# Five expert pairs written to DRAM and gathered back, weight loads in another order, and three small moves, in a two-layer decoder kernel

## The chip, the cores and the metric

The kernel runs on one core of a Trainium2 chip. A core has TensorE (PE in the profile: matmuls; PEld is its weight load), VectorE (DVE), ScalarE (ACT), GpSimd (POOL) and SyncE (SP); 16 DMA engines move data between DRAM and the on-chip memory SBUF. PSUM holds matmul results. The metric is device time in microseconds (us), lower is better.

## The reference

Two decoder layers over 512 tokens of width 1024. Each layer has a mixer (stick-breaking attention and gated linear attention) and then a mixture of 32 SwiGLU experts with hidden width 256, of which each token uses the two best of one group. A vector `c` gives shift, scale and gate of both sub-layers (adaLN).

```python
def reference(x, c, w_ada, b_ada, norm_mix, norm_ffn, ...):
    c_act = jax.nn.silu(c)
    for l in range(DEPTH):
        mod = (c_act @ w_ada[l] + b_ada[l])[:, None, :]
        shift_m, scale_m, gate_m, shift_f, scale_f, gate_f = jnp.split(mod, N_MOD, axis=-1)
        h = rms_norm(x, norm_mix[l]) * (1.0 + scale_m) + shift_m
        x = x + gate_m * hybrid_mixer(h, w_in[l], ...)
        h = rms_norm(x, norm_ffn[l]) * (1.0 + scale_f) + shift_f
        x = x + gate_f * hierarchical_moe(h, w_router_grp[l], ..., w_gate[l], w_up[l], w_down[l])
    return x
# in hierarchical_moe, for each group g:
    a = jnp.einsum('nd,edf->nef', hf, w_gate[g])
    u = jnp.einsum('nd,edf->nef', hf, w_up[g])
    y = y + jnp.einsum('nef,efd->nd', jax.nn.silu(a) * u * comb[:, g, :, None], w_down[g])
```

## The kernel before

The expert stage `moe` runs once in each layer. Its tokens are sorted into slots: each expert has 64 slots, two experts make a pair of 128 slots, and there are 16 pairs, numbered from 0. `logits` transposes the tokens (tiles `xT`, copied out of PSUM by DVE) and multiplies them with the router's weights; DVE then picks group and experts and counts slots (`slot`). Meanwhile ACT writes the normed tokens (`xn`) and GpSimd's queue sends them to DRAM (`xg`). `fetch` gathers the 128 rows of a pair from `xg` by an indirect DMA of GpSimd; empty slots fetch nothing. `gather` transposes them (`g`, `gT`).

For pair i, PE then runs three kinds of work. `hidden` multiplies the pair's tokens with gate and up weights of both experts (I call this gu(i); its weights are tile `wgu`, 2 MiB for an expert, 5 buffers). `turn` transposes the hidden values. `down` multiplies them with the down weights (d(i); tile `wd`, 1 MiB for an expert, 4 buffers), and DVE scales the result by routing weight and gate (`o`). `combine` brings the rows back to their tokens: ACT and GpSimd split `o` into a high and a low part (`ohi`, `olo`), and PE multiplies both with a 0/1 matrix `oT` made by `places`, into 8 pieces `y` of 128 tokens by 512 columns, 16 matmuls (y(i)); DVE adds the pieces to `x`. The order on PE in the loop is d(i-1), gu(i), y(i-1), the latter mixed with transposes for later pairs.

All weights come by SP's queue, which issues in program order. The list `queue` fixes that order; an entry (0, e) is the gate and up weights of expert e, (1, e) its down weights. Nine entries are asked for before the stage begins (five of `wgu`, four of `wd`, 14 MiB); each later one waits for a buffer that gu or d has let go. The scheduler of the framework orders the instructions inside an engine, within what the code pins (`kept_dma`, `pm`).

At the start of layer 0, `mixer` loads x, the rows of small vectors (`load_rows`: biases and norm gains, transposed by PE into `cols`) and the adaLN weights (`wada`), squares x on ACT, and projects.

Of the kernel before, what the change touches and what calls it, by code (L numbers as in the profile page):

```python
# [9 lines left out]
F = mybir.dt.float32  # L10
R = mybir.dt.float32r
BF = mybir.dt.bfloat16
I32 = mybir.dt.int32
# [7 lines left out]
P = 128  # L21
# [2 lines left out]
SBW, GKW, GVW, RANK, NIN = 512, 256, 512, 16, 3088  # L24
NE, FE, CAP = 32, 256, 64
NX = 16


@with_exitstack
def hybrid_decoder_kernel(ctx, tc, x, c, w_ada, b_ada, norm_mix, norm_ffn, w_in, w_gk2, b_gk, q_gain,  # L30
# [36 lines left out]
    def att(name="att"):  # L67
        return bank(name, "att", 3)
# [17 lines left out]
    def kept_dma(eng, o, a):  # L86

        tc.keep_in_program_order(eng.dma_start(o, a))
# [98 lines left out]
    def load_rows():  # L187

        rows = rowt[0]([100, P], name="rows")
        for l in range(L):  # L190
            for i in range(2):
                r = 32 * l + 16 * i
                kept_dma(SY, rows[r:r + 16], b_ada[l, 3 * D * i:3 * D * i + 2 * D].rearrange("(r p) -> r p", p=P))
        kept_dma(SY, rows[64:80], norm_mix.rearrange("l (k p) -> (l k) p", p=P))
        kept_dma(SY, rows[80:96], norm_ffn.rearrange("l (k p) -> (l k) p", p=P))
        kept_dma(SY, rows[96:100], b_gk.rearrange("l (g p) -> (l g) p", p=P))
# [14 lines left out]

    xs = dram.tile([S, D], F, name="xs")
    xg = dram.tile([S, D], F, name="xg")

    mod = [const.tile([P, 6, KT], F, name=f"mod{l}") for l in range(L)]
    gates, gms, rowt = {}, {}, {}
# [66 lines left out]
    def mixer(l, xt, ss, x_src, pool, later):  # L283
# [42 lines left out]
        lrT = const.tile([RANK, S], F, name="lrT", tag="lrT")  # L326


        if l == 0:
            for tt in range(NT):  # L330
                for q in range(2):
                    square(ss, xt, tt, q)
        if l:

            ps = att("warm")
            for _ in range(16):
                pm(ps[:, 0:P], ident, ident, True, True)
        pin = tiny.tile([P, 1], F, name="pin")
        A.copy(pin, ss[:, 0, 0:1])
        tc.keep_in_program_order(A.preload_act_table_set("natural_log_exp_and_others"))  # L340
        rs = inv_rms(ss, G if l else A)
        xn = []
        for tt in range(NT):
            t = xt[tt // 2][:, tt % 2]
            xn.append(t if l == 0 else mixs([P, D], name="xn"))
            if l == 0:
                V.tensor_scalar(xn[tt], t, rs[:, tt:tt + 1], None, op0=OP.mult)
            else:
                V.tensor_scalar(xn[tt][:, 0:512], t[:, 0:512], rs[:, tt:tt + 1], None, op0=OP.mult)
                A.activation(xn[tt][:, 512:D], t[:, 512:D], AF.Copy, scale=rs[:, tt:tt + 1])  # L350
        if l:

            for i in range(2):
# [487 lines left out]
    def logits(l, xt, s2):  # L841


        wr, lc, _ = route[l]
        lgT = misc("lgT")
        for k in range(KT):
            ps = att("xT")
            for tt in range(NT):
                T.transpose(ps[:, P * tt:P * tt + P], xt[tt // 2][:, tt % 2, P * k:P * k + P], ident)
            t = s2([P, S], name="xT")  # L850
            V.tensor_copy(t, ps)
            o = 64 * (k % 2)
            mm(lgT[o:o + 64], wr[:, 36 * k:36 * k + 64], t, k < 2, k >= KT - 2)
        t = s2([P, S], name="lgT")
        V.tensor_copy(t, lgT)
        lg = route[l][2] = att("lg")[:, 0:NT * 36].rearrange("p (t e) -> p t e", t=NT)
        for tt in range(NT):
            mm(lg[:, tt], t[:, P * tt:P * tt + P], two_parts, tt == 0, True)

    def moe(l, xt, ss, pool):  # L860
        wgu = slots(pool, "wgu", 5, 16384)
        wd = slots(pool, "wd", 4, 8192)
        g4 = slots(pool, "gT", 3, 4096)
        rows_ = slots(pool, "rows", 4, 4096)
# [28 lines left out]
        wr, lc, lg = route.pop(l)  # L893
        rs = inv_rms(ss)

        for tt in range(NT):
            xn = rows_([P, KT, P], name="xn")
            normed = A.activation(xn, xt[tt // 2][:, tt % 2].rearrange("t (p k) -> t k p", k=KT), AF.Copy,
                                  scale=rs[:, tt:tt + 1])
# [137 lines left out]
        def down(hT, ws, i=None):  # L1037

            n = len(ws)
            r = slice(0, 64 * n)  # L1040
            parts, last = [], None
            if i == NE // 2 - 1:

                last = wgu([P, 2, 2, 512], R, name="last")
            for q in range(2):
                pd = bank("d", "dy", 4)
                for j in range(2):
                    for e in range(n):
                        pm(pd[64 * e:64 * e + 64], hT[:, j, 64 * e:64 * e + 64],
                           ws[e][:, D * j + 512 * q:D * j + 512 * q + 512], j == 0, j == 1)  # L1050
                o = ot([P, 512], name="o")
                gate = gates[l, 5][r, 512 * q:512 * q + 512]
                if i is None:
                    V.tensor_tensor(o[r], pd[r], gate, op=OP.mult)
                    parts.append(o)
                else:
                    V.scalar_tensor_tensor(o, pd, cws[:, i:i + 1], gate, op0=OP.mult, op1=OP.mult)  # L1057
                    if last is not None:
                        hi, lo = last[:, q, 0], last[:, q, 1]
                    else:  # L1060
                        hi, lo = ohl([P, 512], R, name="ohi"), ohl([P, 512], R, name="olo")
                    A.activation(hi, o, AF.Copy)  # L1062
                    (G if last is None else V).tensor_tensor(lo, o, hi.bitcast(F), op=OP.subtract)  # L1063
                    parts.append((hi, lo))
            return parts
# [29 lines left out]
        def combine_last(pairs):  # L1095
# [17 lines left out]
            yield  # L1113
            for n, u in ((0, 5), (0, 6), (1, 0), (1, 1), (0, 7), (1, 2), (1, 3), (1, 4), (1, 5), (1, 6), (1, 7)):
                unit(n, u)

        def spread(slot, slot0):

# [80 lines left out]
        with tc.issue_after(listed.ins), tc.issue_after(normed.ins):  # L1199
# [14 lines left out]
            V.tensor_tensor(e2, e2, den, op=OP.mult)  # L1214
            V.tensor_tensor(cw[:, :, 1:2], e2, gw, op=OP.mult)
            dump(f"cw{l}", cw)
            exw = tmp.rearrange("p t k e -> p (t k) e")
            V.tensor_tensor(exw, ex.rearrange("p t k e -> p (t k) e"), cw.rearrange("p t k -> p (t k)")[:, :, None].to_broadcast([P, NT * 2, NE]), op=OP.mult)
        cws = pool.tile([P, NE // 2], F, name="cws")
# [17 lines left out]
        for _ in rest:  # L1237
            pass
        gT1, second = gather(fetched[1:2])
        hs = None  # L1240
        for i in range(NE // 2):
            while not {(0, 2 * i), (0, 2 * i + 1)} <= set(loaded):
                load_weights(1)
            if i % 2 == 0:
                now = gT
                if i < NE // 2 - 2:
                    gT, rest = gather(fetched[i + 2:i + 4])
                    fetched += [fetch(idx[:, j:j + 1]) for j in range(i + 4, min(i + 6, NE // 2))]

            if i:  # L1250
                part = places(i - 1), down(hT, [loaded.pop((1, e)) for e in (2 * i - 2, 2 * i - 1)], i - 1)
            *_, hs = hidden(gT1 if i == 1 else now, 0 if i < 2 else P * (i % 2), [loaded.pop((0, e)) for e in (2 * i, 2 * i + 1)])
            load_weights(4)
            if i == 1:
                overflow_lists()
            if i == NE // 2 - 1:
                break

            if i == 0:
                for _ in second:  # L1260
                    pass
                weights_by_slot()
            for u in range(4):
                for v in range(2):
                    if i:
                        combine(2 * u + v, *part)
                next(rest, None)
                if u == 2:
                    hT = turn(hs)
        last = []  # L1270
        end = combine_last([part, last])
        next(end)
# [93 lines left out]
```

## Time and profile before

| | us |
|---|---|
| median of 3 runs | 1230.94 (1230.35 to 1233.77) |
| profiled execution, its own time | 1231.71 |
| its span, first to last instruction | 1229.6 |
| PE busy | 1176.4 (96%) |
| DVE busy | 687.8 (56%) |
| ACT busy | 472.6 (38%) |
| POOL busy | 188.2 (15%) |

The profile is one execution. Busy shares are averages over stages with different limits: the expert stages lie at about 350 to 630 us (layer 0) and 940 to 1230 us (layer 1), and in them the DMA engines are busy all the time as well.

### The profile page before, as it was taken

Reading aid. Unit: us, or ns where it says so; the run is one execution under the profiler, and the core shown is the slowest. Engines: PE = TensorE matmul, PEld = TensorE weight load, DVE = VectorE, ACT = ScalarE, POOL = GpSimd, SP = SyncE. Lnnn points to the kernel's source line nnn. Section 1 sums busy time; section 2 is a strip of 40 time slices with the busy share of each in tenths; the row PEclk is TensorE's granted clock in tenths of the full one; section 3 lists DMA queues with packets and bytes.
Section 4 is the critical chain, followed back from the end, with each engine's and each line's share of the span. In section 5 each row is a group of like instructions: output and inputs, shape, how many; then the busy total and the mean of one; then the engine's idle time right before and its main releaser. Section 6 shows DMA issues by size and latency. Waiting matters only on the chain. (4 is left out here: it accounts for less than half of the span.)

```text
span 1229.6 us, 17212 instructions
## 1 busy us (share of the span) xinstructions
PE 1176.4 (96%) x6441; PEld 743.4 (60%) x6441; DVE 687.8 (56%) x1343; ACT 472.6 (38%) x940; POOL 188.2 (15%) x222
## 2 busy tenths in 40 slices
PE   4999999999989999999999997999999999999996
PEld 2687766666765444444478785666776744444443
DVE  4475545465864555555566563445846565555553
ACT  4376646453242111111155764454624411111111
POOL 1000010011302222221110001001310222222110
PEclk8999999999999999999999999999999999999999
DMA  9653665643687999999445354564129599999981
GB/s 299 211 181 110 202 166 155 198 152 96 258 353 265 410 411 420 420 419 418 178 168 167 96 172 108 171 179 127 56 103 383 212 397 420 420 418 420 420 328 69
DMA packets 105902, 312.27 MB, mean 254 GB/s; under 512 B 12852, under 2 KB 49912, under 8 KB 81240
## 3 DMA queue, kind: packets, MB, share of 16 engines
q1 hardware_dynamic: 96920, 289.62, 63.3%
q0 software_dynamic: 8896, 21.52, 5.2%
q8 instruction: 52, 0.85, 0.3%
q14 instruction: 34, 0.28, 0.1%
HBM read 311.08 MB, written 8.40 MB: 260 GB/s over the span
## 5 line engine op out<-in xcount | busy, mean ns | idle before, releaser
L78 PE MATMUL gu<-wgu,gT 128*64 128x512 f32 x1024 | 225.4, 592 | 0.1
L74 PE MATMUL proj<-whl,hh 128*128 128x512 f32 (+2 forms) x768 | 220.6, 370 | 0.1
L78 PEld LDWEIGHTS gu<-wgu,gT 128*64 128x64 f32 x1024 | 75.4, 137 | 143.7 <-issue 142.2
L74 PEld LDWEIGHTS proj<-whl,hh 128*128 128x128 f32 x768 | 133.9, 190 | 35.0 <-issue 13.3
L1070 DVE TENSOR_TENSOR x<-y,x 128x512 f32<-128x512 f32 x240 | 148.2, 679 | 0.9 <-PE y L78 0.9
L74 PE MATMUL proj<-whl,hl 128*128 128x512 f32 (+2 forms) x384 | 138.6, 362 | 0.0
L1025 DVE TENSOR_TENSOR hs<-hs,gu 128x256 f32<-128x256 f32 x32 | 13.5, 421 | 201.2 <-ACT hs L1024 201.2
L78 PE MATMUL d<-wd,hT 128*64 128x512 f32 x512 | 116.9, 598 | 1.4 <-ACT hT L1034 1.4
L1063 POOL TENSOR_TENSOR olo<-o,ohi 128x512 fp32r<-128x512 f32 x60 | 77.0, 1285 | 263.4 <-ACT ohi L1062 263.4
L96 DVE TENSOR_TENSOR whl<-raw,whl 128x512 fp32r<-128x512 f32 (+2 forms) x128 | 73.2, 574 | 78.0 <-ACT whl L95 67.6
L78 PE MATMUL y<-ohi,oT 128*128 128x512 f32 x240 | 104.5, 436 | 0.0
L95 ACT ACTIVATE whl<-raw 128x512 fp32r<-128x512 f32 (+2 forms) x128 | 66.4, 524 | 76.6 <-PE proj L74 64.7
L78 PE MATMUL y<-olo,oT 128*128 128x512 f32 x240 | 94.2, 393 | 0.0
L74 PEld LDWEIGHTS proj<-whl,hl 128*128 128x128 f32 x384 | 72.4, 189 | 14.2 <-issue 4.3
L1024 ACT ACTIVATE hs<-gu 128x256 f32<-128x256 f32 x32 | 12.3, 385 | 168.4 <-PE gu L78 168.4
L78 PEld LDWEIGHTS d<-wd,hT 128*64 128x64 f32 x512 | 33.9, 136 | 62.2 <-issue 48.1
L78 PEld LDWEIGHTS y<-ohi,oT 128*128 128x128 f32 x240 | 45.4, 189 | 31.7 <-issue 26.0
L1003 ACT ACTIVATE gT<-g,mod 128x256 f32<-128x256 f32 (+1 forms) x72 | 39.0, 544 | 62.6 <-DVE gT L1005 62.3
L1062 ACT ACTIVATE ohi<-o 128x512 fp32r<-128x512 f32 x60 | 37.8, 630 | 61.7 <-DVE o L1057 61.7
L1057 DVE SCALAR_TENSOR_TENSOR o<-d,cws,gate_f 128x512 f32<-128x512 f32 x64 | 47.6, 746 | 21.4 <-PE d L78 21.4
L733 POOL TENSOR_TENSOR raw<-raw,gate_m 128x1024 f32<-128x1024 f32 x16 | 40.4, 2533 | 122.9 <-DMA raw<-in_w_out_dram 63.1
L78 PE MATMUL ada<-wada,ct 128*32 128x512 f32 x320 | 50.2, 600 | 5.3 <-DMA wada<-in_w_ada_dram 3.8
(332 smaller groups left out, 1935.0 us busy)
## 6 DMA issues: line engine op xcount, KB each, us to landing
wgu<-in_w_gate_dram SPq DMA_DIRECT2D x64, 1024.0 KB, 9.6
wgu<-in_w_up_dram SPq DMA_DIRECT2D x64, 1024.0 KB, 11.8
wd<-in_w_down_dram SPq DMA_DIRECT2D x64, 1024.0 KB, 11.0
wada<-in_w_ada_dram SPq DMA_DIRECT2D x96, 512.0 KB, 5.1
raw<-in_w_in_dram SPq DMA_DIRECT2D x80, 256.0 KB, 4.5
raw<-in_w_out_dram SPq DMA_DIRECT2D x16, 512.0 KB, 5.0
raw<-in_w_in_dram SPq DMA_DIRECT2D x32, 128.0 KB, 4.0
xg<-xn POOLq DMA_DIRECT2D x8, 512.0 KB, 5.9
```

The costliest lines, as they stand in the source:

```text
L74: T.matmul(o, a, b, start=start, stop=stop, skip_group_check=True)
L78: tc.keep_in_program_order(T.matmul(o, a, b, start=start, stop=stop, skip_group_check=True))
L95: A.activation(hi, src, AF.Copy)
L96: eng.tensor_tensor(lo, src, hi.bitcast(F), op=OP.subtract)
L733: G.tensor_tensor(t, t, gates[l, 2][:, None, cols].to_broadcast([P, 2, 512]), op=OP.mult)
L1003: A.activation(o, src, AF.Identity, scale=m, bias=b)
L1024: A.activation(hs[r], gu[r, 0:256], AF.Silu)
L1025: V.tensor_tensor(hs[r], hs[r], gu[r, 256:512], op=OP.mult)
L1057: V.scalar_tensor_tensor(o, pd, cws[:, i:i + 1], gate, op0=OP.mult, op1=OP.mult)
L1062: A.activation(hi, o, AF.Copy)
L1063: (G if last is None else V).tensor_tensor(lo, o, hi.bitcast(F), op=OP.subtract)
L1070: V.tensor_tensor(xc, ps, xc, op=OP.add)
```

## The change

There are four parts.

1. The first five pairs (`NY = 5`) are not combined by matmuls. Their scaled rows `o` are written to a DRAM tile `ys` by GpSimd's queue. Near the end of the stage, `take_back` gathers each token's row from `ys` by an indirect DMA (8 gathers in a layer: 4 token tiles, two expert choices; a choice outside the first five pairs fetches nothing) and DVE adds it to `x` under a 0/1 mask `ysm`. For these pairs d(i-1) stands behind gu(i).
2. The list `queue` follows the order in which buffers come free, and `rows` buffers stand ahead of `wd` in memory.
3. The small vectors' rows are loaded by GpSimd's queue; x is squared in whole rows; the first normed rows are shared by DVE and ACT; 12 matmuls of a constant run on PE ahead of the first products.
4. The `xT` copies of the router go to DVE and ACT in turn, and one of four `xn` tiles is made by GpSimd.

```diff
-                kept_dma(SY, rows[r:r + 16], b_ada[l, ...])     # and three more of load_rows
+                kept_dma(G, rows[r:r + 16], b_ada[l, ...])
...
+            load_rows()
             xt = [xq([P, 2, D], name="x") for _ in range(2)]
...
-            load_rows()
...
+        ps = att("warm")
+        if l == 0:
+            pm(ps[0:1, 0:1], ss[:, 0, 2:3], ident[:, 0:1], True, True)
+        for _ in range(16 if l else 12):
+            pm(ps[:, 0:P], ident, ident, True, True)
...
-            V.tensor_copy(t, ps)
+            (A.copy if k % 2 else V.tensor_copy)(t, ps)
...
-        queue = [(0, 0), (0, 1), (0, 2), (0, 3), (1, 0), (1, 1), (0, 4), (1, 2), (1, 3)]
-        for i in range(0, NE, 2):
-            queue += [(0, e) for e in (i + 5, i + 6) if e < NE] + [(1, e) for e in (i + 4, i + 5) if e < NE]
+        queue = [(0, 0), (0, 1), (0, 2), (0, 3), (0, 4), (1, 0), (1, 1), (1, 2), (1, 3)]
+        freed = [(0, 0)]
+        for i in range(1, NE // 2):
+            freed += [(0, i), (1, i - 1)] if i <= NY else [(1, i - 1), (0, i)]
+        for w, i in freed:
+            queue += [(w, e) for e in ((2 * i + 4, 2 * i + 5) if w else (2 * i + 5, 2 * i + 6)) if e < NE]
...
+                    if i < NY:
+                        kept_dma(G, ys[P * i:P * i + P, 512 * q:512 * q + 512], o)
+                        continue
...
+        def take_back(tt, k):
+            r = rows_([P, D], name="back")
+            G.indirect_dma_start(r, None, ys[:, :], bass.IndirectOffsetOnAxis(ap=ysi[:, tt, k:k + 1], axis=0),
+                                 bounds_check=NY * P - 1, oob_is_err=False)
+            xc = xt[tt // 2][:, tt % 2]
+            return lambda: V.scalar_tensor_tensor(xc, r, ysm[:, tt, k:k + 1], xc, op0=OP.mult, op1=OP.add)
...
-            if i:
+            if i > NY:
                 part = places(i - 1), down(hT, [loaded.pop((1, e)) for e in (2 * i - 2, 2 * i - 1)], i - 1)
...
+            if i <= NY:
+                if i:
+                    hT = turn(hs)
+                for _ in range(4):
+                    next(rest, None)
+                if i:
+                    down(hT, [loaded.pop((1, e)) for e in (2 * i - 2, 2 * i - 1)], i - 1)
+                    load_weights(2)
+                hs = new
+                if i == NY:
+                    hT = turn(hs)
+                continue
```

SP's queue at the start of the program before: the input c, x, the small vectors' rows, then the first adaLN weights.

```order
L185 DMA cT<-in_c_dram 128x8
L88 DMA x<-in_x_dram 128x1024 x4
L88 DMA rows<-in_b_ada_dram 16x128 x4
L88 DMA rows<-in_norm_mix_dram 16x128
L88 DMA rows<-in_norm_ffn_dram 16x128
L88 DMA rows<-in_b_gk_dram 4x128
L88 DMA wada<-in_w_ada_dram 128x4x256 x4
```

The same place now: the seven loads of `rows` have gone to GpSimd's queue, and the adaLN weights follow x at once.

```order
L187 DMA cT<-in_c_dram 128x8
L90 DMA x<-in_x_dram 128x1024 x4
L90 DMA wada<-in_w_ada_dram 128x4x256 x4
L409 DMA raw<-in_w_in_dram 128x2x256 x2
L90 DMA wada<-in_w_ada_dram 128x4x256 x4
```

SP's queue in layer 1's expert stage, before: the down weights of experts 8 and 9, gate and up of 11 and 12, the down weights of 10 and 11 (which d(5) needs), gate of 13. Eight experts' gate and up loads stand between the first release and the last `wd` row shown here.

```order
L880 DMA wd_9195<-in_w_down_dram 128x2048
L880 DMA wd_9197<-in_w_down_dram 128x2048
L884 DMA wgu_9297<-in_w_gate_dram 128x2048
L884 DMA wgu_9297<-in_w_up_dram 128x2048
L884 DMA wgu_9300<-in_w_gate_dram 128x2048
L884 DMA wgu_9300<-in_w_up_dram 128x2048
L880 DMA wd_9303<-in_w_down_dram 128x2048
L880 DMA wd_9305<-in_w_down_dram 128x2048
L884 DMA wgu_9413<-in_w_gate_dram 128x2048
```

The same place now: between the down weights of 8 and 9 and those of 10 and 11 stand gate and up of experts 13 and 14. Ten experts' gate and up loads now stand ahead of the down weights of 10 and 11.

```order
L889 DMA wd_9070<-in_w_down_dram 128x2048
L889 DMA wd_9072<-in_w_down_dram 128x2048
L893 DMA wgu_9102<-in_w_gate_dram 128x2048
L893 DMA wgu_9102<-in_w_up_dram 128x2048
L893 DMA wgu_9105<-in_w_gate_dram 128x2048
L893 DMA wgu_9105<-in_w_up_dram 128x2048
L889 DMA wd_9144<-in_w_down_dram 128x2048
L889 DMA wd_9146<-in_w_down_dram 128x2048
L893 DMA wgu_9168<-in_w_gate_dram 128x2048
```

GpSimd's queue in layer 1's expert stage now: one `xn`, the four writes of `xg`, gathers of `rows`, and among them ten writes of `ys` (two for each of five pairs); the eight gathers `back` stand further down, between the last `olo`. Before, the first ten `olo` stood where the `ys` writes stand.

```order
L909 TENSOR_TENSOR xn<-x,rs 128x1024
L90 DMA xg<-xn 128x1024 x4
L989 DMA rows<-xg,idx 128x1024 x8
L90 DMA ys<-o 128x512 x4
L989 DMA rows<-xg,idx 128x1024 x2
L90 DMA ys<-o 128x512 x4
L989 DMA rows<-xg,idx 128x1024 x2
L90 DMA ys<-o 128x512 x2
L1078 TENSOR_TENSOR olo<-o,ohi 128x512 x4
```

So of GpSimd's work ten subtractions in a layer are replaced by ten issues of writes, and eight indirect gathers are added.

## Rows read from the trace of the kernel before

**Rows 1.** The page: DMA rates in 40 slices of the span.
```profile
GB/s 299 211 181 110 202 166 155 198 152 96 258 353 265 410 411 420 420 419 418 178 168 167 96 172 108 171 179 127 56 103 383 212 397 420 420 418 420 420 328 69
```

**Rows 2.** The chain that ended last, layer 1: start us, us, what.
```profile
1043.99 3.58 PE d L78 x16
1047.58 6.87 PE gu L78 x32
1054.44 1.12 PE y L78 x4
...
1058.31 0.92 PE y L78 x4
1059.45 3.58 PE d L78 x16
```

**Rows 3.** Windows of 10 us, layer 1's expert stage; last columns PE clock, DMA share, GB/s.
```profile
990.00:1000.00 10.00, 10.00 (x52) 5.46 (x49) 6.91 (x13) 1.79 (x4) 2.75 (x3) 1.00 0.97 382
...
1050.00:1060.00 10.00, 10.00 (x52) 5.57 (x50) 5.07 (x10) 1.23 (x3) 0.87 (x2) 1.00 1.01 421
...
1190.00:1200.00 10.00, 10.00 (x48) 5.03 (x46) 5.93 (x11) 0.76 (x2) 0.00 (x0) 1.00 0.37 149
```

**Rows 4.** SP's timeline, layer 1: first weight load after the stage began, and expert 14's last.
```profile
976.64 0.33 SPq L884 DMA_DIRECT2D wgu<-in_w_gate_dram  x1
...
1040.34 0.42 SPq L884 DMA_DIRECT2D wgu<-in_w_up_dram  x1
```

**Rows 5.** DMA issues of two short stretches, 1032 to 1033 and 1040.2 to 1040.8; last number us to landing.
```profile
wd<-in_w_down_dram SPq DMA_DIRECT2D x2, 1024.0 KB, 12.2
...
wgu<-in_w_up_dram SPq DMA_DIRECT2D x1, 1024.0 KB, 14.3
```

**Rows 6.** Window of 2 us in which only the output is written, rows of 2 KB.
```profile
1220.00:1222.00 2.00, 0.31 (x2) 0.00 (x0) 2.00 (x4) 0.00 (x0) 0.00 (x0) 1.00 1.04 382
```

**Rows 7.** Layer 1's mixer: PE's timeline around its longest idle time there, then windows of 1 us.
```profile
759.17 0.61 PE L490 MATMUL kT<-ident,two 128*128 128x128 f32 x4
766.05 1.11 PE L497 MATMUL qT<-ident,two 128*128 128x128 f32 x4 [6.28 <-ACT w L550]
...
763.00:764.00 1.00, 0.00 (x0) 0.00 (x0) 0.00 (x0) 0.00 (x0) 1.00 (x3) 0.64 0.90 260
769.00:770.00 1.00, 1.00 (x4) 0.67 (x3) 1.00 (x2) 0.63 (x1) 0.00 (x0) 0.50 0.00 0
770.00:771.00 1.00, 1.00 (x10) 0.27 (x10) 0.93 (x3) 0.63 (x1) 0.00 (x0) 0.95 0.00 0
```

**Rows 8.** SP's timeline at the start of the program.
```profile
1.20 1.84 SPq L88 DMA_DIRECT2D x<-in_x_dram  x4
3.08 2.05 SPq L88 DMA_DIRECT2D rows<-in_b_ada_dram  x4
...
10.54 1.66 SPq L88 DMA_DIRECT2D wada<-in_w_ada_dram  x3
```

**Rows 9.** PE's timeline at the start, then a window of 2 us.
```profile
12.73 0.40 PE L198 MATMUL cols<-ident,rows 100*128 100x100 f32 x1 [12.73 <-DVE sm L278]
...
18.08 1.08 PE L74 MATMUL ada<-wada,ct 128*32 128x256 f32 x8
...
24.61 1.20 PE L74 MATMUL proj<-whl,hh 128*128 128x512 f32 x2
...
24.00:26.00 2.00, 2.00 (x10) 1.29 (x14) 2.00 (x4) 1.60 (x3) 0.00 (x0) 0.50 1.10 349
```

**Rows 10.** Layer 1, from the router to the experts: timelines of DVE and POOL.
```profile
949.88 0.69 DVE L851 COPY xT<-xT 128x512 f32<-128x512 f32 x1 [2.31 <-PE xT L849]
...
958.29 0.53 POOL L88 DMA_DIRECT2D xg<-xn  x1 [1.53 <-ACT gd L1201]
963.79 1.07 POOL L977 DMA_INDIRECT rows<-xg,idx  x1 [4.96 <-DVE dg L1229]
```

**Rows 11.** The page's groups: scaling of 128 by 512 results on DVE.
```profile
L1057 DVE SCALAR_TENSOR_TENSOR o<-d,cws,gate_f 128x512 f32<-128x512 f32 x64 | 47.6, 746 | 21.4 <-PE d L78 21.4
```

More of the change, by code (lines that the diff above doesn't have):

```diff
@@ L26 @@
 NX = 16
+NY = 5
 @with_exitstack
@@ L192, in load_rows @@
                 r = 32 * l + 16 * i
[L193 to L196, printed above, removed]
+                kept_dma(G, rows[r:r + 16], b_ada[l, 3 * D * i:3 * D * i + 2 * D].rearrange("(r p) -> r p", p=P))
+        kept_dma(G, rows[64:80], norm_mix.rearrange("l (k p) -> (l k) p", p=P))
+        kept_dma(G, rows[80:96], norm_ffn.rearrange("l (k p) -> (l k) p", p=P))
+        kept_dma(G, rows[96:100], b_gk.rearrange("l (g p) -> (l g) p", p=P))
         ps = misc("cols")
@@ L213, in hybrid_decoder_kernel @@
     xg = dram.tile([S, D], F, name="xg")
+    ys = dram.tile([NY * P, D], F, name="ys")
     mod = [const.tile([P, 6, KT], F, name=f"mod{l}") for l in range(L)]
@@ L326, in mixer @@
         lrT = const.tile([RANK, S], F, name="lrT", tag="lrT")
+        pin = tiny.tile([P, 1], F, name="pin")
         if l == 0:
+            V.memset(ss[:, 1], 0.0)
             for tt in range(NT):
-                for q in range(2):
-                    square(ss, xt, tt, q)
-        if l:
[L335 to L340, printed above, removed]
+                junk = s2([P, D], BF, name="junk")
+                A.activation(junk, xt[tt // 2][:, tt % 2], AF.Square, accum_out=ss[:, 0, tt:tt + 1])
+                if tt == 0:
+                    A.copy(pin, ss[:, 0, 0:1])
+                    tc.keep_in_program_order(A.preload_act_table_set("natural_log_exp_and_others"))
+        ps = att("warm")
[3 more added lines that the diff above has]
+            pm(ps[:, 0:P], ident, ident, True, True)
+        if l:
+            A.copy(pin, ss[:, 0, 0:1])
+            tc.keep_in_program_order(A.preload_act_table_set("natural_log_exp_and_others"))
         rs = inv_rms(ss, G if l else A)
@@ L345, in mixer @@
             xn.append(t if l == 0 else mixs([P, D], name="xn"))
[L346 to L350, printed above, removed]
+            V.tensor_scalar(xn[tt][:, 0:512], t[:, 0:512], rs[:, tt:tt + 1], None, op0=OP.mult)
+            A.activation(xn[tt][:, 512:D], t[:, 512:D], AF.Copy, scale=rs[:, tt:tt + 1])
         if l:
@@ L861, in moe @@
         wgu = slots(pool, "wgu", 5, 16384)
+        rows_ = slots(pool, "rows", 4, 4096)
         wd = slots(pool, "wd", 4, 8192)
         g4 = slots(pool, "gT", 3, 4096)
-        rows_ = slots(pool, "rows", 4, 4096)
         ot = slots(pool, "o", 2, 2048)
@@ L894, in moe @@
         rs = inv_rms(ss)
-        for tt in range(NT):
+        for tt in (3, 0, 1, 2):
             xn = rows_([P, KT, P], name="xn")
-            normed = A.activation(xn, xt[tt // 2][:, tt % 2].rearrange("t (p k) -> t k p", k=KT), AF.Copy,
-                                  scale=rs[:, tt:tt + 1])
+            src = xt[tt // 2][:, tt % 2].rearrange("t (p k) -> t k p", k=KT)
+            if tt == 3:
+                tc.keep_in_program_order(G.tensor_tensor(xn, src, rs[:, tt:tt + 1, None].to_broadcast([P, KT, P]), op=OP.mult))
+            else:
+                normed = A.activation(xn, src, AF.Copy, scale=rs[:, tt:tt + 1])
             kept_dma(G, xg[P * tt:P * tt + P, :], xn.rearrange("t k p -> t (k p)"))
@@ L1050, in down @@
                            ws[e][:, D * j + 512 * q:D * j + 512 * q + 512], j == 0, j == 1)
-                o = ot([P, 512], name="o")
+                o = (ohl if i is not None and i < NY else ot)([P, 512], name="o")
                 gate = gates[l, 5][r, 512 * q:512 * q + 512]
@@ L1216, in moe @@
             dump(f"cw{l}", cw)
+            V.tensor_scalar(ysi, slot, 65535.0, None, op0=OP.min)
+            V.tensor_scalar(ysm, slot, float(NY * P), None, op0=OP.is_lt)
             exw = tmp.rearrange("p t k e -> p (t k) e")
@@ L1239, in moe @@
         gT1, second = gather(fetched[1:2])
-        hs = None
+        hs, back, taken = None, [(tt, k) for tt in range(NT) for k in range(2)], []
         for i in range(NE // 2):
@@ L1248, in moe @@
                     fetched += [fetch(idx[:, j:j + 1]) for j in range(i + 4, min(i + 6, NE // 2))]
-            if i:
+            if i > NY:
                 part = places(i - 1), down(hT, [loaded.pop((1, e)) for e in (2 * i - 2, 2 * i - 1)], i - 1)
-            *_, hs = hidden(gT1 if i == 1 else now, 0 if i < 2 else P * (i % 2), [loaded.pop((0, e)) for e in (2 * i, 2 * i + 1)])
-            load_weights(4)
+            *_, new = hidden(gT1 if i == 1 else now, 0 if i < 2 else P * (i % 2), [loaded.pop((0, e)) for e in (2 * i, 2 * i + 1)])
+            load_weights(2 if i <= NY else 4)
             if i == 1:
@@ L1262, in moe @@
                 weights_by_slot()
+            if i <= NY:
[6 more added lines that the diff above has]
+                    load_weights(2)
+                hs = new
+                if i == NY:
+                    hT = turn(hs)
+                continue
+            hs = new
             for u in range(4):
                 for v in range(2):
-                    if i:
-                        combine(2 * u + v, *part)
+                    combine(2 * u + v, *part)
+                if i >= NE // 2 - 4 and u % 2 == 0:
+                    taken.append(take_back(*back.pop(0)))
+                    if len(taken) > 1:
+                        taken.pop(0)()
                 next(rest, None)
@@ L1269, in moe @@
                     hT = turn(hs)
+        for (tt, k) in back:
+            taken.append(take_back(tt, k))
+        for add_back in taken:
+            add_back()
         last = []
```

1 line of the change is left out of this document (added).

## The prediction, made before the changed kernel ran

> **What bounds the kernel now.** I read the page's slices first, then the chain of waits, then windows of the expert stage. PE is busy for 96% of the span, and the chain is PE throughout the expert stage, so PE looks like the bound. But the row of DMA rates stands at 410 to 420 GB/s in the slices of both expert stages and nowhere else for long [rows 1]. The chain in layer 1 shows the period of one pair: d takes 3.58 us, gu 6.87, and the y phase runs from 1054.44 to 1059.45, 5.01 us, of which four pieces of y are 1.12 + 0.94 + 0.92 + 0.92 = 3.90 (the first and the last of the four stand in the rows) [rows 2]. That is 15.46 us. In the same stretch DMA is busy with a share of 1.01 at 421 GB/s [rows 3]. A pair needs 6 MiB of weights, 6.29 MB, and its 64 to 128 gathered rows, 0.26 MB on the mean (1024 rows of 4 KB over 16 pairs). At 421 GB/s that is 15.6 us. So two engines stand at their limit with nearly one period. DMA never starves from the first release at 976.64 [rows 4] until the weights run out shortly after 1190, where the rate is down to 149 [rows 3]. What PE gains in the stage is worth only as much as DMA follows.
>
> **The y matmuls taken out.** Five pairs lose 3.90 us each, 19.5 us of PE time in a layer, 39 in both. Their cost on ACT, POOL and DVE (splitting, adding) lies beside PE and gives nothing back.
>
> **What takes their place: the wait for weights.** After the first release SP's queue asks, in the new order, for ten experts' gate and up (20 MiB) and eight down weights (8 MiB), and the last of these 28 MiB are the down weights of experts 10 and 11, which d(5) needs. Before, the same 28 MiB end with expert 14's up weights. Those were issued at 1040.34 [rows 4] and took 14.3 us [rows 5], so they were there at 1054.6. Asking earlier helps little, since DMA was busy all the time: only the dip of 990 to 1000 (382 against 421, some 0.9 us of work) [rows 3] can be filled by a fuller queue. So they come at 1053.7, if nothing else is moved. The down weights of 10 and 11 were there at about 1032.5 + 12.2 = 1044.7 before [rows 5] and waited for PE; now PE waits for them.
>
> Something else is moved: `ys`. Five pairs write 128 x 4 KB each, 2.62 MB, in rows of 2 KB, and all of it before d(5). The nearest row is the output's writing, rows of 2 KB as well, at 382 GB/s with DMA at 1.04 [rows 6]: 6.9 us. Below, the writes cost nothing if they fit in gaps; but a share of 1.01 has none. Above I take twice the price, 13.8. I take 6.9, as the output's rows are the same shape. The Trainium skill (DMA: Bandwidth & Descriptors, Issuing engines are not separate DMA queues) says the same of the queues: what GpSimd issues runs on the same 16 engines as SP's loads and interleaves. If it were not so, the term would be 0.
>
> So d(5) can start at 1053.7 + 6.9 = 1060.6. Before, it started at 1059.45 [rows 2]. From d(5) on, pairs have their full y phases again and PE goes at 15.46 us as before. **The whole saving of PE's 19.5 us is thus spent in waiting, and the stage ends 1.2 us later** (from 5.7 earlier, if writing is free, to 8 later).
>
> **The clock after the wait.** Without y, PE would be at d(4) by about 1037 and gets its weights (22 of 28 MiB) at some 976.6 + 22/28 x 77 + 5 = 1042; then d(5) is waited for from about 1046 to 1060, 14 us. The nearest row is an idle PE in layer 1's mixer: idle from 759.8 to 766.05, granted clock 0.64 in the us from 763, still 0.50 (1.2 of 2.4 GHz) in the us before 770 and 0.95 after [rows 7]. So 4.0 us of work ran at half rate, 2.0 us lost. The wait here is longer, so the same is due: d(5) at 3.58 us and a piece of gu(6) run at 1.2 GHz. I take 2.0, between 0 and 2.5. Together 3.2 us a layer, and 6.4 for two (layer 0 runs the same code with the same sizes).
>
> **Reading back.** About 5/16 of 1024 rows, 1.3 MB, is 3.4 us of DMA at 382 GB/s [rows 6], late, where weights come well ahead of need; nothing. Eight additions of 128 x 1024 on DVE at twice 746 ns [rows 11], 12 us a layer, lie in pairs 11 to 14, where DVE is busy 5 to 6 of 10 us [rows 3]; nothing. If a gather comes late, DVE stands in order with y's additions behind it, and PE soon waits for PSUM: bounded by one landing, some 5 us. Ten writes take the place of ten `olo` on POOL's queue; gathers stand behind them, but run two pairs ahead.
>
> **From router to experts.** The first gathers start at 963.79, 5.5 us after the last of `xg` was issued at 958.29 [rows 10]; with one `xn` on GpSimd and buffers free sooner, `xg` no longer ends last, and two engines copy `xT`. On the other side DVE has the overflow lists' counting ahead of the first `gT` now, and one of its operations ahead of `idx`. I take a gain of 1.0 a layer (between -0.5 and 2), which moves the first release too: -2.0.
>
> **The start.** SP is held by the seven small loads: x is issued at 1.20 and the first adaLN weights at 10.54 [rows 8]; the first ada products end at 19.2, and the projection starts at 24.61 [rows 9]. Now the weights follow x. DMA must bring x and the first four of them, 4.2 MB; at the 349 GB/s of this stretch [rows 9] that is 12 us, so they are there by 15 instead of some 18 to 20. `cols` still needs the small rows, now from GpSimd's queue, at about 11 to 13; then come 12 warm-up matmuls (2 us). I expect the projection 2 to 3 us earlier. PE ran from 24 to about 29 at a clock of 0.50 [rows 9], 2.5 us lost; the warm-up may save some. After that DMA, at 349, bounds again: 12.6 MB of x and the first group need 36 us. I take -3.0 (from -1 to -5).
>
> **Sum.** 1231.71 + 6.4 - 2.0 - 3.0 = 1233.1 against the profiled execution's own time. That execution was 0.8 us above the median, so 1232.3 for the median. 0.3% (3.7 us) is about what a measurement of this kernel can tell from no change; this lies inside it.
>
> **Rivals.**
> *The wait costs less* (faster). The writes fit in at half price (3.4 us), the clock loss is hidden by a wait that follows it, start and router give their upper ends: 2 x (1053.7 + 3.4 - 1059.45) = -4.7, -4, -5: 1217. A third of this can be told from no change. For it: the bounds of three terms; against it: each must go the same way. Chance 0.24.
> *DMA is not at its limit* (faster by much). The windows before show a share of 1.01 at 421 GB/s, and 1.04 was reached elsewhere [rows 3, 6]; a queue that is always full might draw 421 x 1.04 / 1.01 = 433. 28 MiB then take 67.8 us, with 6.9 for writes and some 2 us of latency d(5) starts at 1053.3, 6 us earlier in each layer, and the sum is 1230.9 - 12.3 + 4 - 2 - 3 = 1218; with no DMA bound at all, 1231 - 39 - 5 = 1187. Against it: 410 to 420 in every full slice of both stages [rows 1]. Chance 0.05. The Trainium skill (DMA: Bandwidth & Descriptors, Where 436 GB/s comes from) puts the fabric's ceiling at 435 GB/s, close to this.
> *The lead is gone* (slower). Before, down weights were there 15 us ahead of d(5); now every later pair starts with what just came, and 15.6 us of DMA stand against 15.46 of PE. If the loads' rate beside writes and gathers falls below about 405 GB/s, a pair takes 16.2 and waits return in pairs 6 to 14: 9 x 0.7 = 6 us; the read-back's 3.4 us is then paid too. At twice the price for writes, 6.9 more. One of these in both layers gives 1240 to 1250. For it: the balance of 15.6 and 15.46; against it: after d(5) the buffers for two pairs are full. Chance 0.30.
> *My forecast* (inside 0.3%): 0.41, with its own range 1227 to 1235.
>
> So faster 0.29, same 0.41, slower 0.30. For 8 in 10 I cut a tenth on either side: 1219 to 1244.
>
> **What would show it.** In the pairs' stage after: an idle PE of 10 to 15 us ahead of the sixth d in each layer, ended by down weights (by their landing); granted clock 0.5 there for some 4 us; DMA at 415 to 425 from the first release on without a dip; the last d where it was before within 5 us. At the start, `wada` issued at 3 us and the first `proj` near 22. The prediction is wrong if the sixth d starts well before 1055, counted from a first release at 976.6, or if PE waits again for weights in pairs 8 to 14, or if DVE waits for `back`.

## The result and the profile after

The changed kernel takes 1240.66 us, the median of five runs (1238.04 to 1243.06), against 1230.94 for the kernel before in the same session: a ratio of 1.0075, 95% interval 1.0053 to 1.0097. It is slower, by 9.2 us (6.5 to 11.9) by that ratio; the two medians lie 9.7 apart. The profiled execution of after is its shortest run, 1238.04 us with a span of 1236.3.

The page after, the rows that answer to [rows 1]: how busy the engines are, then PE's busy tenths, its granted clock and the DMA rates in 40 slices.

```profile
PE 1148.3 (93%) x6307; PEld 723.5 (59%) x6307; DVE 653.5 (53%) x1256; ACT 460.8 (37%) x922; POOL 203.1 (16%) x247
...
PE   5999999999989949999999998999999997799995
...
PEclk9999999999999989999999998999999999899998
...
GB/s 319 249 119 130 184 173 178 162 180 103 278 319 300 421 421 421 419 419 419 212 188 155 87 193 86 172 187 120 68 129 415 210 412 422 421 419 419 419 347 69
```

DMA stands at 412 to 422 GB/s in the full slices of both expert stages, much as before; PE has a hole where each stage is a third through (a 4, and 7 7), and the granted clock is down there (an 8 each). PE is busy 28 us less than before, and the kernel is longer.

PE's timeline in layer 1 around the sixth down product, without the weight loads; it answers to [rows 2].

```profile
1044.07 3.65 PE L80 MATMUL d<-wd,hT 128*64 128x512 f32 x14 [1.35 <-DMA wd<-in_w_down_dram]
1047.65 0.50 PE L1044 MATMUL hsT<-ident,hs 128*128 128x128 f32 x2
1059.12 1.94 PE L80 MATMUL d<-wd,hT 128*64 128x512 f32 x2 [10.97 <-DMA wd<-in_w_down_dram]
1061.51 3.80 PE L80 MATMUL d<-wd,hT 128*64 128x512 f32 x13 [0.46 <-DMA wd<-in_w_down_dram]
...
1077.56 3.65 PE L80 MATMUL d<-wd,hT 128*64 128x512 f32 x16
```

PE idles 11 us, until the down weights of experts 10 and 11 land. Two of the 16 matmuls run with expert 10's; the rest starts at 1061.51, where the kernel before started d(5) at 1059.45. (13 in a row; the sixteenth runs after the first matmul of the next gate and up product.)

Windows of after in layer 1 (columns as in [rows 3]), then SP's timeline in the same stretch.

```profile
975.00:985.00 10.00, 10.00 (x90) 6.33 (x90) 4.81 (x12) 4.19 (x9) 0.98 (x1) 1.00 0.88 347
985.00:995.00 10.00, 10.00 (x52) 3.92 (x50) 2.92 (x5) 1.78 (x4) 3.15 (x4) 1.00 0.91 356
...
1054.00:1058.00 4.00, 0.00 (x0) 0.00 (x0) 0.00 (x0) 0.00 (x0) 0.00 (x0) 0.50 1.01 424
1058.00:1062.00 4.00, 2.42 (x4) 0.58 (x6) 0.00 (x0) 0.00 (x0) 0.00 (x0) 0.50 1.02 424
1062.00:1066.00 4.00, 4.00 (x18) 1.22 (x16) 0.97 (x2) 0.63 (x1) 0.44 (x1) 0.91 1.01 418
```

```profile
975.03 0.33 SPq L893 DMA_DIRECT2D wgu<-in_w_gate_dram  x1
...
976.35 0.71 SPq L893 DMA_DIRECT2D wgu<-in_w_up_dram  x1
987.04 0.33 SPq L893 DMA_DIRECT2D wgu<-in_w_gate_dram  x1
...
1053.06 13.73 SPq L889 DMA_DIRECT2D wd<-in_w_down_dram  x4
```

While PE idles, the weights come at 424 GB/s. The clock is 0.50 (1.2 GHz) from 1054 to 1062. At the start of the stage the rate dips to 347 and 356: SP asked for two experts by 976.35, and for nothing more until the second gate and up product let go of its buffers at 987.04.

I count each stage from the start of its first gate and up product to the start of its last down product: **241.83 us in either layer before**, 246.45 and 247.05 after. Those 9.8 us are the loss inside the stages. The same count for every run stands in the table below. In layer 1 the 5.2 us divide into 3.7 up to the sixth down product (counted from its main part, at 1061.51), 0.6 from there to the seventh, and 0.9 from the seventh to the last; in layer 0 into 3.2, 0.6 and 0.9.

### The profile page after: what moved, and what is told of

The parts are those of the page before. It is cut to its first block, busy times and chain, and to the rows that moved or that the text cites. A ratio compares the mean times of both kernels' runs of the same rounds, so it can differ in the third digit from the quotient of the medians.

```text
span 1236.3 us, 16928 instructions
## 1 busy us (share of the span) xinstructions
PE 1148.3 (93%) x6307; PEld 723.5 (59%) x6307; DVE 653.5 (53%) x1256; ACT 460.8 (37%) x922; POOL 203.1 (16%) x247
## 5 line engine op out<-in xcount | busy, mean ns | idle before, releaser
L80 PE MATMUL gu<-wgu,gT 128*64 128x512 f32 x1024 | 229.5, 593 | 2.0 <-DMA wgu<-in_w_up_dram 1.7
L76 PE MATMUL proj<-whl,hh 128*128 128x512 f32 (+2 forms) x768 | 218.1, 367 | 0.1
L80 PE MATMUL d<-wd,hT 128*64 128x512 f32 x512 | 127.8, 614 | 32.7 <-DMA wd<-in_w_down_dram 31.5
L1085 DVE TENSOR_TENSOR x<-y,x 128x512 f32<-128x512 f32 x160 | 99.7, 683 | 0.9 <-PE y L80 0.9
L97 ACT ACTIVATE whl<-raw 128x512 fp32r<-128x512 f32 (+2 forms) x128 | 66.6, 524 | 82.8 <-PE proj L76 67.4
L1036 ACT ACTIVATE hs<-gu 128x256 f32<-128x256 f32 x32 | 12.3, 385 | 209.9 <-PE gu L80 209.9
L1078 POOL TENSOR_TENSOR olo<-o,ohi 128x512 fp32r<-128x512 f32 x40 | 53.9, 1353 | 147.9 <-ACT ohi L1077 147.8
L80 PE MATMUL y<-ohi,oT 128*128 128x512 f32 x160 | 70.0, 437 | 0.4 <-DVE x L1085 0.4
L80 PE MATMUL y<-olo,oT 128*128 128x512 f32 x160 | 63.0, 394 | 0.0
L989 POOL DMA_INDIRECT rows<-xg,idx x32 | 33.7, 1053 | 117.3 <-PE g L1009 102.3
L1077 ACT ACTIVATE ohi<-o 128x512 fp32r<-128x512 f32 x40 | 25.2, 630 | 71.1 <-DVE o L1069 71.0
```

What stands on the lines that cost most here:

```text
L76: T.matmul(o, a, b, start=start, stop=stop, skip_group_check=True)
L80: tc.keep_in_program_order(T.matmul(o, a, b, start=start, stop=stop, skip_group_check=True))
L97: A.activation(hi, src, AF.Copy)
L989: G.indirect_dma_start(r, None, xg[:, :], bass.IndirectOffsetOnAxis(ap=idx, axis=0), bounds_check=S - 1, oob_is_err=False)
L1085: V.tensor_tensor(xc, ps, xc, op=OP.add)
```

## The experiments

All ratios are to the kernel before, from 4 to 12 runs of the kernel against 23 to 29 of before in the same session (after: 5 against 5). Runs that are compared with each other below come in part from different sessions, so a difference of two ratios carries both intervals.

| run | stage, layer 0 | layer 1 | ratio (95%) |
|---|---|---|---|
| before | 241.83 | 241.83 | 1 |
| after | 246.45 | 247.05 | 1.0075 (1.0053 to 1.0097) |
| e1_moves | 242.25 | 242.23 | 0.9987 (0.9974 to 1.0000) |
| e2_route | 247.40 | 248.80 | 1.0121 (1.0102 to 1.0140) |
| e3_no_read_back | 246.83 | 246.78 | 1.0068 (1.0048 to 1.0089) |
| e4_no_route | 239.94 | 241.07 | 0.9965 (0.9946 to 0.9985) |
| e5_one_pair | 243.66 | 241.12 | 0.9970 (0.9953 to 0.9987) |
| e6_two_pairs | 240.78 | 240.93 | 1.0000 (0.9978 to 1.0022) |
| e7_old_order | 243.98 | 244.53 | 1.0046 (1.0030 to 1.0063) |
| e8_kept_warm | 245.97 | 246.60 | 1.0064 (1.0039 to 1.0090) |
| e9_less_weights | 237.55 | 239.23 | 0.9951 (0.9933 to 0.9968) |
| e10_less_weights_before | 241.84 | 241.83 | 1.0005 (0.9993 to 1.0017) |
| e11_one_pair_mended | 239.70 | 239.68 | 0.9966 (0.9942 to 0.9990) |
| e12_one_write | 241.83 | 241.83 | 0.9977 (0.9960 to 0.9994) |

The stages are of one profiled execution each, the ratios of all runs. My theory was the prediction's: transfers bound the stage, and each byte ahead of the sixth down product costs its time. The rivals: the read-back and its additions, the order of loads, the clock, or the small moves are the cost.

**The two halves of the change (e1, e2).** e1 takes only the small moves of the diff (`load_rows`, squares and warm-up, `logits`, `xn`), e2 all the rest.

> The kernel before with the small moves alone (rows by GpSimd's queue, the logits' copies on two engines, one block of normed rows on GpSimd), all experts as before. Theory (the way by DRAM loses what these gain): the first expert product of layer 0 comes about 4 us sooner, that of layer 1 another 2 us, and both stay to the end: 1225 us, a ratio near 0.995. Rival (the moves gain nothing at the end, because weights or the mixer take it back): a ratio of 0.999 to 1.002. Rival (the moves cost, by the later first projection at 27.4 us): above 1.003.

> The kernel before with the way by DRAM and the new order of loads alone, without the small moves. Theory: the route costs 6 to 7 us a layer for the rows written and about 1 us for the clock after the wait, less nothing for the placements left out: 13 to 15 us, 1244 to 1246, a ratio near 1.012. Rival (the small moves are the cost, the route is even): a ratio of 0.998 to 1.003.

The route alone costs 14.9 us (12.5 to 17.2): the theory's figure, but in part by luck. In its profile 12.5 us lie in the two stages and 2.4 at the end of the span (see e12), a term that the theory did not have. The moves alone gain 1.6 (0 to 3.2), about a quarter of what I expected; that they gain nothing is not excluded. The two halves add up to 13.3 us, against 9.2 for the whole change; within the three intervals that difference is not shown to be real.

**Reading back and writing (e3, e4).** e3 leaves out the first part of this diff, e4 both parts.

```diff
-                if i >= NE // 2 - 4 and u % 2 == 0:
-                    taken.append(take_back(*back.pop(0)))
...
-        for add_back in taken:
-            add_back()
```
```diff
-                        kept_dma(G, ys[P * i:P * i + P, 512 * q:512 * q + 512], o)
```

> The changed kernel without the fetch of the rows back from DRAM and without the eight additions by VectorE; the rows are still written. It leaves out the first ten experts' share of the sum. Theory (the read-back is hidden but for a wait in the fourteenth pair of layer 1): 0 to 2 us under the changed kernel in all, 1238 to 1241, a ratio to the kernel before near 1.007. Rival (the late part pays: transfers of the read-back push the last weights and the additions hold back the last output blocks): 4 to 8 us under it, a ratio of 1.001 to 1.004.

> The changed kernel with neither the rows written to DRAM nor fetched back; the products and their scaling stay, the order of loads and the wait too. It leaves out the first ten experts' share of the sum. Theory (DMA is full, so 2.62 MB a layer push the weights by 6 to 7 us): the sixth pair's down product 6 to 7 us sooner in each layer, 12 to 14 us in all: 1226 to 1229, a ratio of 0.996 to 0.999, and the wait ahead of it stays at 5 us or so. Rival (writes fit beside the loads; the loss is the order of loads and the clock): within 3 us of the kernel without the read-back.

Without the reading the ratio falls by 0.0007, 0.9 us, far inside the intervals. From e3 to e4, the writes alone, the stages fall by 6.9 and 5.7 us and the ratio by 0.0103, 12.7 us (some 3.5 either way; 1.5 of it lie at the end of the span, see e12). For 5.24 MB the stages' 12.6 us make 416 GB/s: the writes take the time of so many bytes of weights. PE's waits in the first half of layer 1's stage (us in total, times, longest), e4 first and then after:

```profile
PE d L80 <- DMA wd<-in_w_down_dram: 10.7, 3, 9.8
```
```profile
PE d L80 <- DMA wd<-in_w_down_dram: 16.0, 6, 11.0
```

Even with writes at no cost, e4 has its wait, 9.8 us at the longest where I expected 5, and 39 us less of PE work make the two stages only 2.7 us shorter.

**How many pairs (e5, e6).** `NY = 1` and `NY = 2` in the changed kernel.

> The changed kernel with one pair by way of DRAM instead of five. Theory (the weights' lead decides, some 5.7 us at the sixth pair's down product in the kernel before): 3.9 us of placements saved against 1.3 us of writes use up 5.2 us of that lead, so no long wait comes: 3 to 4 us a layer are kept beside what the small moves gain, 1219 to 1223, a ratio of 0.991 to 0.995. Rival (every saving on TensorE turns into waiting, whatever its size): the ratio of the small moves alone or above, 0.998 to 1.001.

> The changed kernel with two pairs by way of DRAM. Theory (the lead decides): 7.8 us saved and 2.5 us of writes use up 10.3 us, 4.6 us more than the lead, so waits of 4 to 5 us appear and a layer gains 0 to 3 us: a ratio of 0.993 to 0.999, above or at that of one pair. Rival (what five pairs cost is a fixed price of the route, not a price per row written): at 1.003 or above.

0.9987, 0.9970, 1.0000, 1.0075 for no, one, two and five pairs. One pair was expected at 0.995 or below and missed it. Its profile shows a new wait in the second pair, 2.1 us in layer 0, on a low part of GpSimd, whose slot a write to DRAM still held. PE and GpSimd in e5, layer 0:

```profile
410.31 0.50 PE L80 MATMUL y<-olo,oT 128*128 128x512 f32 x1 [2.15 <-POOL olo L1078]
```
```profile
396.97 0.56 POOL L90 DMA_DIRECT2D ys<-o  x1 [1.14 <-DVE o L1069]
...
409.00 1.26 POOL L1078 TENSOR_TENSOR olo<-o,ohi 128x512 fp32r<-128x512 f32 x1 [7.50 <-DMA ys<-o]
```

The write issued at 396.97 holds its buffer until some 409. For two pairs the waits for down weights were there (3.2 and 3.4 us, 4 to 5 expected), and 1.0000 lies just above the expected 0.993 to 0.999: its stages are 1.0 us shorter each, and GpSimd's DRAIN at the end of the span (see e12) takes 1.7 longer.

**The order of loads (e7).**

```diff
-            freed += [(0, i), (1, i - 1)] if i <= NY else [(1, i - 1), (0, i)]
+            freed += [(1, i - 1), (0, i)]
...
-            load_weights(2 if i <= NY else 4)
+            load_weights(4 if i > NY else 0 if i else 2)
...
-                    load_weights(2)
+                    load_weights(4)
```

> The changed kernel with the loads queued as in the kernel before, the down weights of a pair ahead of the next gate and up weights, all five pairs still by way of DRAM. Theory (28 MiB ahead of the sixth down product set its wait): 24 MiB stand ahead of it and 26 ahead of the seventh pair's gate and up product, so one wait of 14 us splits in two with a product between them; 3 to 8 us a layer come back: a ratio of 0.995 to 1.003. Rival (DMA is full, so the order moves only the place of the wait): within 0.002 of the changed kernel's 1.0075.

0.0029 below the changed kernel, 3.6 us, between the two expectations, and 2.5 us in each stage. The waits stand ahead of gate and up products now, 8.3 us in all in layer 1 where down products waited 16.0:

```profile
PE gu L80 <- DMA wgu<-in_w_up_dram: 8.3, 3, 4.4
```

So the new order has a price of its own, a little under the 3 us a layer expected as the least. Its profile also has a wait on GpSimd's low part as in e5 (2.0 us in layer 1, 0.4 in layer 0), so the order's own price may be somewhat higher. Most of the loss isn't the order's.

**The clock (e8).** `keep_warm(ident, 44)` behind `hT = turn(hs)` for `i == NY`.

> The changed kernel with 44 idle products of the identity (about 10.5 us) on TensorE ahead of the sixth down product, which write a bank that nobody reads, so that its clock doesn't fall in the wait. Theory: the product after the wait and the first of the next runs at full clock, 2 us a layer: a ratio near 1.004. Rival (the clock's loss lies beside a later wait for weights): no change, 1.0075.

A window inside the wait in layer 1 (columns as in [rows 3]), then PE's timeline:

```profile
1054.00:1058.00 4.00, 2.05 (x12) 1.01 (x10) 0.00 (x0) 0.00 (x0) 0.00 (x0) 1.00 1.00 416
```
```profile
1058.55 3.22 PE L80 MATMUL d<-wd,hT 128*64 128x512 f32 x13 [1.36 <-DMA wd<-in_w_down_dram]
...
1074.02 2.37 PE L80 MATMUL d<-wd,hT 128*64 128x512 f32 x10
```

The clock stays at 1.00 through the wait. The next down product then comes 15.47 us after the sixth (1058.55 to 1074.02), where it took 16.05 in after (1061.51 to 1077.56). The clock cost 0.6 us a layer, not 2; the stages as a whole are 0.5 us shorter each. The ratio fell by 0.0011, within the intervals.

**Fewer bytes (e9, e10).** From the fifth expert on half of each down weight is loaded and used twice, in the changed kernel and in the kernel before.

```diff
-                SY.dma_start(t, src(w_down).rearrange("(p k) n -> p (k n)", p=P))
+                w = src(w_down).rearrange("(p k) n -> p (k n)", p=P)
+                SY.dma_start(t[:, 0:1024] if half else t, w[:, 0:1024] if half else w)
```

> The changed kernel with half of each down weight loaded from the fifth expert on, the half used twice; all products stay. It leaves out half of 28 down weights a layer, 14.7 MB, some 35 us of transfers. Theory (the saved placements are lost to waiting for weights, and to nothing else): the wait ahead of the sixth down product is gone and the 19.5 us a layer show, from the first gate and up product to the last down product 222 to 225 us: a ratio of 0.968 to 0.974. Rival (the route itself, its writes, GpSimd's issues and the additions, costs what it saves): 0.995 or above.

> The kernel before with the same half loads of the down weights, which leaves out the same part. Theory (TensorE sets the pace of 15.46 us a pair there, the weights keep up with it): nothing is gained, 0.998 to 1.001. Rival (the weights pace the kernel before too): below 0.995.

Before gains nothing (1.0005), as expected: there TensorE paces. After gains 0.0124, 15 us. The theory's 0.968 to 0.974 did not come; 0.9951 lies at the edge of the rival's "0.995 or above". Its account did not come, though: with the writes, GpSimd's issues and the additions all left in, the stages fell by 8.9 and 7.8 us, and the wait for down weights is still the longest. I had counted all 14.7 MB of a layer; only the eight half weights that land ahead of the sixth down product count, 8 x 0.524 = 4.19 MB, 10.0 us at 420. PE in e9, layer 1:

```profile
1028.93 3.99 PE L80 MATMUL d<-wd,hT 128*64 128x512 f32 x16
...
1043.13 6.80 PE L80 MATMUL d<-wd,hT 128*64 128x512 f32 x15 [9.77 <-DMA wd<-in_w_down_dram]
```

The sixth product comes 82.8 us after the first gate and up product, not 93.6, and gives some 3 us back by running wholly at the low clock (6.80 for 15 matmuls, at a granted clock of 0.54 from 1040 to 1050, where the fifth product's 14 in after took 3.65). What is saved ahead of that product stays to the end.

**One pair, mended (e11).** `NY = 1`, and the second pair's low parts in other slots:

```diff
+ (s2 if i == NY else ohl)([P, 512], R, name="olo")
```

> The kernel with one pair by way of DRAM, where the second pair's low parts go into other slots than the buffers that the two writes hold for some 12 us. Theory (in the run with one pair the second pair's placements wait 2.1 and 1.2 us for that, and the clock falls after it): 2 to 4 us in layer 0 and 1 to 2 in layer 1 come back: a ratio of 0.992 to 0.995. Rival (a wait for weights takes the place): 0.997 as without the mend.

The wait on GpSimd is gone and the stages are 2.1 us shorter than before, both. The ratio, 0.9966, misses the expected 0.992 to 0.995 and does not tell e11 from e5, whose profile is its slowest run; what e5's wait cost over all its runs is not shown. The rival's account (a wait for weights takes the place) did not come either: PE waits for no weights in e11's two stages. GpSimd's DRAIN at the end of the span takes 1.6 us longer than before here (see e12), which the expectation did not count. Both e5 and e11 beat the kernel before, by about 4 us (intervals in the table); that this is more than the moves alone gain shows in the stages, not in the ratios.

**The end of the span (e12).** From the last packet of the output to the end of the span the profiles without the route (before, e1, e4, e10, e12) show 3.5 to 3.6 us, those with it (after, e2, e3, e5 to e9, e11) 5.0 to 7.1. The expectation below has 3.5 to 5.0 and 7.0 to 8.5; I had read them from slices such as these and taken the low ones (29, 25, 20 in after) for empty, but they still hold rows of the output. DMA rates in the last 20 us, 0.5 us a slice, of e1 and of after:

```profile
GB/s 0 0 0 0 0 0 0 0 0 33 0 0 0 0 0 0 0 0 0 0 90 385 49 307 389 377 389 381 361 393 389 381 303 16 0 0 16 0 0 0
```
```profile
GB/s 0 0 0 0 0 0 0 0 0 0 0 356 168 217 381 369 377 373 369 397 356 356 377 74 29 25 20 0 16 0 16 0 0 0 0 0 0 0 0 0
```

```diff
+                    if l == 0 and i == 8:
+                        kept_dma(G, ys[:, 512 * q:512 * q + 512], o)
```

> The kernel with the small moves alone, and two writes of 0.26 MB by GpSimd's queue to a new DRAM buffer in layer 0's ninth pair, which nobody reads. Theory (the time from the last output transfer to the end of the span, 3.5 to 5.0 us in the kernels without that buffer and 7.0 to 8.5 in those with it, belongs to such writes): 7 us or more there, and a ratio of 1.000 to 1.003. Rival (it varies by chance, or goes with the amount written): 5 us or less, 0.998 to 1.000.

3.6 us: two writes to a new buffer don't make it. The instruction records show where the time goes. After the output GpSimd's sequencer runs an instruction DRAIN, and the other engines wait for it; the last of the three figures is the longest one in ns, before and then after:

```profile
L1362 POOLq DRAIN  x3: 51/103/1855, 1226.9 to 1229.3; - x3
```
```profile
L1410 POOLq DRAIN  x3: 51/103/4877, 1230.6 to 1236.0; - x3
```

It goes with the number of DMAs that GpSimd issued in the whole program: 1.86 us for 78 (before, e10), 1.94 for 85 (e1, e4), 2.10 for 87 (e12), 3.41 for 105 (e3, e5, e11), 3.57 for 109 (e6), 4.22 for 114 (e2), 4.88 for 121 (after, e7 to e9). It does not go with their bytes: e3 issues 20 writes and no gathers back, e5 4 writes and 16 gathers, and both have 3.41. The change adds 43 such DMAs (20 writes, 16 gathers, 7 small loads). Why the instruction takes longer then is open.

## Why the prediction was off, step by step

The range held the time, but in part by luck: its likeliest case, within 0.3% of before, did not come. 1240.66 lies in the range of the slower rival ("the lead is gone"), yet its mechanism did not come either: once the sixth down product is done PE waits for no weights in either layer, and the writes cost their single price.

- **The saving is wholly spent in waiting: right.** e4 shows it for free writes, e9 and e10 from the side of the bytes; a run without any wait was not made. "DMA is not at its limit" is out: the rates stayed at 416 to 426 from 1005 to 1061.5.
- **Writes at 6.9 us a layer: right.** Measured 6.9 and 5.7 by the stages, 6.2 and 6.4 by the sixth down product, from e3 to e4. The Trainium skill (DMA: Bandwidth & Descriptors, Issuing engines are not separate DMA queues), which has GpSimd's transfers interleave with SP's on the same 16 engines, agrees with e3 against e4.
- **Weights at 1053.7 + 6.9: mis-sized, and the step that failed first.** From the first release (976.64 before, [rows 4]; 975.03 after) to the sixth down product I had 84.0 us; it took 86.5 in layer 1, and 85.9 in layer 0. The failing step is "only the dip can be filled by a fuller queue": it booked 0.9 us gained, and nothing new ahead of that product but the writes. At first the dip got deeper: 347 and 356 GB/s, where the kernel before has 351 and 383 in the first two windows from its release (share 0.89 in the first, so "DMA never starves" and "busy all the time" did not hold there either). Later windows made up for it. What moved from the first release to the last of the 28 MiB, before (976.64 to 1054.60) and then after (975.03 to 1061.51):

```profile
DMA packets 4853, 31.35 MB, mean 402 GB/s; under 512 B 889, under 2 KB 889, under 8 KB 1170
```
```profile
DMA packets 6007, 34.87 MB, mean 403 GB/s; under 512 B 1241, under 2 KB 1241, under 8 KB 2266
```


The mean rate is the same, so some 0.2 us were gained and not 0.9. Of the 3.5 MB more, 2.62 are the writes (6.5 us at 403), and 0.9 MB, 2.2 us, the prediction did not have: gathers, of which seven were issued in this time and five before (0.43 MB), and more of the weights behind (0.48 MB). That is the 2.5 us: 0.7 and 2.2 more, 0.4 less.
- **Clock, 2.0 a layer: mis-sized,** 0.6 by e8. Two matmuls with expert 10's weights ran at 1059.12, inside the wait for expert 11's, so part of the slow stretch cost nothing.
- **Reading back at nothing: wrong by 0.7 a layer.** From the seventh down product to the last it is 137.4 us in after (1077.56 to 1214.97), 136.7 in e3 (1076.76 to 1213.48) and 136.5 before. All of the difference to e3 lies between the thirteenth and the fourteenth down product: 16.17 us in each of the eight kernels that read back, 15.46 to 15.48 in the six that don't. (Over the whole stage after and e3 differ by -0.4 and +0.3 us, as their waits ahead of the sixth product differ too.) In the fourteenth pair the chain leaves PE for DVE:

```profile
1182.98 0.68 DVE x L1085
1183.66 0.78 DVE x L1140
1184.45 0.33 issue
1184.77 0.69 DVE x L1085
1185.46 0.46 DVE gT L1017
1185.92 0.03 issue
1185.95 0.57 ACT gT L1015
```

An addition (L1140) stands in DVE's order ahead of a piece of y and of the copy `gT`, and PE waits behind. The prediction's "busy 5 to 6 of 10 us" came from other windows: from 1180 to 1190 DVE is busy for 7.85 us before, and for 9.25 in e3 without any addition.

- **Router -2.0 and start -3.0: smaller.** Over eleven profiles with the moves and three without, layer 0's first product comes at 372.2 and 373.9 on the mean, and the time from layer 0's last down product to layer 1's first product is 349.9 and 352.1: -1.7 and -2.2 (which holds the last placements and the mixer too, and scatters by 4 us). By runs e1 gives -1.6, with 3.2 as its far end. At the start the projection did not come near 22 but at 27.43. `wada` was issued at 3.08, as expected, and the first adaLN products ended 2 us earlier than before, at 17.0, but PE wasn't fed behind them:

```profile
11.47 4.54 PE L80 MATMUL warm<-ident 128*128 128x128 f32 x24
15.94 1.07 PE L76 MATMUL ada<-wada,ct 128*32 128x256 f32 x16
...
21.19 0.61 PE L76 MATMUL adaT<-sel,row 128*128 128x1 f32 x4 [3.59 <-ACT row L248]
...
27.43 0.74 PE L76 MATMUL proj<-whl,hh 128*128 128x512 f32 x2
```
```profile
19.73 1.15 ACT L97 ACTIVATE whl<-raw 128x512 fp32r<-128x512 f32 x2 [4.54 <-DMA raw<-in_w_in_dram]
20.78 0.35 ACT L248 COPY row<-ada 128x256 f32<-128x256 f32 x1
```

ACT's copy `row`, which `adaT` needs, stands behind two splits (`whl`) that wait for their weights `raw` until 19.73. In the kernel before, the first two copies ran at 19.28 and 21.70 and the first split at 21.97: the order on ACT has changed. The warm-up matmuls also took 4.5 us, not 2. The projection runs at full clock then (1.00 from 26 to 28), which [rows 9] did not.

- **The end of the span: no term at all;** +3.0, GpSimd's DRAIN (4.88 us against 1.86).

The sum of what was measured, 9.8 - 3.9 + 3.0 = 8.9 us, stands against the 9.2 of the runs; the prediction had 6.4 - 5.0 + 0 = 1.4. The stages were 3.4 too cheap, the moves 1.1 too good, and 3.0 was not seen. The 3.9 is a mean over all profiles; in the two profiles of before and after alone the moves gain 6.2, and 9.8 - 6.2 + 3.1 = 6.7 is the difference of their spans. So the closeness of 8.9 to 9.2 is good to a few us only.

## What to carry to other kernels

Where two engines run at nearly one period, taking work from one buys only the slack of the other: count the bytes that must land ahead of the first instruction after the shortened stretch, and add those that the change itself moves. A saving that drains a lead of a few buffers is worth at most that lead, so try it at its smallest size first. An operation that fits an engine's idle share can still stand ahead of an urgent one in its order. Count the DMAs that a change has GpSimd issue, too: 43 more came here with 3.0 us more at the end of the program.

## What was not expected of the hardware

- Loads and GpSimd's writes together hold 416 to 426 GB/s for 56 us on end (share 1.01 to 1.02); a write of 0.26 MB beside them takes 6.3 to 12.3 us to land, which the buffer behind it feels.
- With halved down weights the kernel before (e10) moves 342 to 362 GB/s in the full slices of its stages and takes the same time: there PE's pace set the rate, and not DMA.
- From the last packet of the output to the end of the span pass 3.5 to 7.1 us, more than half of it GpSimd's DRAIN, which takes 1.86 us after 78 DMAs issued by GpSimd and 4.88 after 121.
